# A max-pooling kernel whose first load becomes short and contiguous

## The chip, the cores and the metric

One core of a Trainium2 chip. The metric is the device time of one execution in microseconds. A profile has its own time, a little off the median of the others; where a profile is explained, its own time is used.

## The reference

```python
x: (32, 256, 4096) float32            # 134.2 MB
for i in range(256):                  # windows of 16 elements
    result[:, :, i] = np.max(x[:, :, 16*i : 16*i + 16], axis=-1)
# result: (32, 256, 256) float32      # 8.4 MB
```

Seen from one of the 128 partitions of the on-chip memory: 16,384 windows come in, 64 bytes each, and 16,384 floats go out.

## The kernel before

One area of 53,200 floats per partition holds three slots for loads, which shrink from the bottom up, and all results, which grow from the top down. So the stores can wait until every load has been issued. The loads and stores go through one queue, in program order. A load waits for the reduction that frees its slot.

```python
    AREA = 53200
    SLOTS = 3
    MOST = 65536 // (4 * W)          # 1024 windows: a row of 64 KB per partition
    ROUNDS_A = 3
    LAST = 4
    # ... sizes: three loads per round, as large as the room left allows
    # = 1024 x3, 980 x3, 924 x3, 868 x3, 816 x3, 768 x3, 244
    groups = [sizes[: ROUNDS_A * SLOTS], sizes[ROUNDS_A * SLOTS :]]
    # ...
    for g, loads in enumerate(groups):
        n = sum(loads)
        xg = xw[first : first + P * n].rearrange("(p n) w -> p (n w)", p=P)
        # ... cut: og, base, b
        for i, size in enumerate(loads):
            a = b - size
            at = n_loads % SLOTS * sizes[n_loads // SLOTS * SLOTS] * W
            slot = area[:, at : at + size * W]
            nc.sync.dma_start(out=slot, in_=xg[:, a * W : b * W])
            nc.vector.reduce_max(out=area[:, base + a : base + b], in_=..., axis=...)
        # ... stores: group 0 whole, group 1 in two parts
    for dst, src in stores:
        nc.sync.dma_start(out=dst, in_=src)
```

A *group* sets where the rows of a load lie in memory. A group of n windows per partition is one contiguous stretch, of which partition p owns n consecutive windows. A load takes a piece of each partition's share, so its 128 rows lie n × 64 bytes apart. In the first group of before n is 8784, so the rows lie 562,176 bytes apart.

## Time and profile before

| | before |
|---|---|
| time, median (range) | 335.48 us (335.36 to 335.57) |
| the profiled execution | 335.70 us, span 333.9 us |
| bytes moved | 134.22 MB read, 8.39 MB written |
| share of the DMA engines | 99.1% |
| VectorE busy | 276.0 us, 83% |

From the page of before: the line of the queue (packets, MB, share of sixteen engines), the bytes of the span, and the group of reductions (busy us, mean ns, idle time and what ended it).

```profile
q1 hardware_dynamic: 3168, 142.61, 99.1%
HBM read 134.22 MB, written 8.39 MB: 427 GB/s over the span
...
L75 DVE TENSOR_REDUCE area<-area 128x1024 f32<-128x16384 f32 (+6 forms) x19 | 276.0, 14525 | 50.0 <-DMA area<-in_x_dram 50.0
```

The transfers fill the span; VectorE is the one that waits. The table of stretches shows how fast they go (stretch, length, VectorE busy, POOL busy, TensorE clock, DMA share, GB/s):

```profile
0.00:23.00 23.00, 0.02 (x1) 0.20 (x4) 1.00 0.99 410
23.00:42.33 19.33, 17.20 (x2) 0.00 (x0) 1.00 1.00 434
300.00:313.00 13.00, 11.43 (x2) 0.00 (x0) 1.00 1.02 439
326.00:331.00 5.00, 0.00 (x0) 0.00 (x0) 1.00 0.95 404
```

A packet is counted in the stretch in which it starts, with its whole length, so short stretches are rough and can exceed 1.00. The second line is a whole load between two landings: 434 GB/s. The Trainium skill, "DMA: Bandwidth & Descriptors", section "Where 436 GB/s comes from", gives 435.2 GB/s as the ceiling of the sixteen ports to the on-chip memory; this trace, just under it, agrees. The same section also says that for transfers between the large memory (HBM) and the on-chip one a smaller ceiling of about 358 GB/s binds; this trace, of one core, does not show it: 434 GB/s.

The timeline of before, first three reductions and the last row (start, length, instruction, idle time before it):

```profile
22.98 17.22 DVE L75 TENSOR_REDUCE area<-area 128x1024 f32<-128x16384 f32 x1 [22.98 <-DMA area<-in_x_dram]
42.33 17.22 DVE L75 TENSOR_REDUCE area<-area 128x1024 f32<-128x16384 f32 x1 [2.13 <-DMA area<-in_x_dram]
61.68 17.22 DVE L75 TENSOR_REDUCE area<-area 128x1024 f32<-128x16384 f32 x1 [2.13 <-DMA area<-in_x_dram]
...
308.79 17.21 DVE L75 TENSOR_REDUCE area<-area 128x768 f32<-128x12288 f32 x2 [1.57 <-DMA area<-in_x_dram]
```

Landings come every 19.35 us, and a reduction of that size takes 17.22. So each reduction sits between two landings and never holds up a transfer.

Each of the sixteen DMA engines moves eight rows of a load. Once under way it takes 2.418 us for a 64 KB row, so eight take 19.34 us. The first reduction starts at 22.98 us, when the last of the sixteen engines has landed its share. 22.98 less 19.34 leaves 3.64 us. Of these, 1.77 us are no loss of an engine: 1.75 pass before the first packet (one row of one engine, as the trace records it) starts, and 0.02 between the last landing and the reduction. The other 1.87 us are the lateness: what the slowest engine lost at the start, its landing included.

### The profile page before, as it was taken

Reading aid. Unit: us, or ns where it says so; the run is one execution under the profiler, and the core shown is the slowest. Engines: PE = TensorE matmul, PEld = TensorE weight load, DVE = VectorE, ACT = ScalarE, POOL = GpSimd, SP = SyncE. Lnnn points to the kernel's source line nnn. Section 1 sums busy time; section 2 is a strip of 40 time slices with the busy share of each in tenths; the row PEclk is TensorE's granted clock in tenths of the full one; section 3 lists DMA queues with packets and bytes.
Section 4 is the critical chain, followed back from the end, with each engine's and each line's share of the span. In section 5 each row is a group of like instructions: output and inputs, shape, how many; then the busy total and the mean of one; then the engine's idle time right before and its main releaser. Section 6 shows DMA issues by size and latency. Waiting matters only on the chain.

```text
span 333.9 us, 109 instructions
## 1 busy us (share of the span) xinstructions
DVE 276.0 (83%) x19; POOL 0.2 (0%) x4
## 2 busy tenths in 40 slices
DVE  0029899798979899897979897979989798988990
POOL 0000000000000000000000000000000000000000
DMA  9898989998999998999999999999999998998997
GB/s 377 377 502 377 495 385 471 392 473 376 473 443 398 474 439 383 425 453 453 446 426 433 426 426 426 426 425 469 407 419 475 395 465 389 465 436 383 448 420 311
DMA packets 3168, 142.61 MB, mean 427 GB/s; under 512 B 352, under 2 KB 352, under 8 KB 352
## 3 DMA queue, kind: packets, MB, share of 16 engines
q1 hardware_dynamic: 3168, 142.61, 99.1%
HBM read 134.22 MB, written 8.39 MB: 427 GB/s over the span
## 4 chain that ended last, share of the span: by engine, by line
DMA 63%; DVE 34%; another core or an unknown queue 1%; issue 0%; SPq 0%
DMA area<-in_x_dram 63%; DVE area L75 34%; SPq L74 0%
## 5 line engine op out<-in xcount | busy, mean ns | idle before, releaser
L75 DVE TENSOR_REDUCE area<-area 128x1024 f32<-128x16384 f32 (+6 forms) x19 | 276.0, 14525 | 50.0 <-DMA area<-in_x_dram 50.0
L108 POOL MEMSET const-bfloat16-1.0<- 128x1 bf16 x1 | 0.1, 102 | 0.0
L108 POOL MEMSET const-uint8-127<- 128x1 uint8 x1 | 0.1, 101 | 0.0
L108 POOL MEMSET const-float32-0.0<- 128x1 f32 x1 | 0.1, 100 | 0.2 <-issue 0.2
L108 POOL MEMSET const-float32-1.0<- 128x1 f32 x1 | 0.1, 99 | 0.0
## 6 DMA issues: line engine op xcount, KB each, us to landing
area<-in_x_dram SPq DMA_DIRECT2D x3, 7840.0 KB, 39.1
area<-in_x_dram SPq DMA_DIRECT2D x3, 7392.0 KB, 36.9
area<-in_x_dram SPq DMA_DIRECT2D x3, 6944.0 KB, 34.7
area<-in_x_dram SPq DMA_DIRECT2D x3, 6528.0 KB, 32.6
area<-in_x_dram SPq DMA_DIRECT2D x3, 6144.0 KB, 30.7
out_dram<-area SPq DMA_DIRECT2D x1, 4392.0 KB, 30.7
out_dram<-area SPq DMA_DIRECT2D x1, 2526.0 KB, 36.3
area<-in_x_dram SPq DMA_DIRECT2D x1, 1952.0 KB, 20.7
```

The source lines that it names most:

```text
L75: nc.vector.reduce_max(out=area[:, base + a : base + b], in_=slot.rearrange("p (n w) -> p n w", w=W), axis=mybir.AxisListType.X,)
L108: nc = _bacc.Bacc("TRN2", target_bir_lowering=False, num_devices=1)
```

## The change

The intent, as the change reads: a first load of 320 windows (20 KB per partition) lets VectorE begin about 13 us earlier and frees the first slot earlier. The short load is made its own group, one contiguous stretch of 2.6 MB. That makes a fourth store. The rest of the sizes are laid out anew: 320, 1024 x2, 996 x3, 936 x3, 880 x3, 828 x3, 780 x3, 756.

```diff
+    FIRST = 320
 ...
-    sizes = []
-    left = total
+    slot_sizes = [MOST]
+    rounds = [[FIRST] + [MOST] * (SLOTS - 1)]
+    left = total - sum(rounds[0])
     while left:
         room = AREA - (total - left)
         n = min(room // (SLOTS * W + SLOTS) // ALIGN * ALIGN, MOST)
-        for _ in range(SLOTS):
+        if left <= slot_sizes[-1]:
+            n = left
+        slot_sizes.append(n)
+        rounds.append([])
+        while left and len(rounds[-1]) < SLOTS:
             n = min(n, left)
-            if n:
-                sizes.append(n)
-                left -= n
-    groups = [sizes[: ROUNDS_A * SLOTS], sizes[ROUNDS_A * SLOTS :]]
+            rounds[-1].append(n)
+            left -= n
+    sizes = [n for r in rounds for n in r]
+    groups = [sizes[:1], sizes[1 : ROUNDS_A * SLOTS], sizes[ROUNDS_A * SLOTS :]]
 ...
-            at = n_loads % SLOTS * sizes[n_loads // SLOTS * SLOTS] * W
+            at = n_loads % SLOTS * slot_sizes[n_loads // SLOTS] * W
 ...
-        if g == 0:
+        if g < len(groups) - 1:
 ...
-    for dst, src in stores:
+    for dst, src in stores[1:2] + stores[0:1] + stores[2:]:
```

## The prediction

> **What bounds the kernel now.** The transfers do. The DMA table gives one queue that fills 99.1% of the sixteen engines' span with 142.61 MB in 333.9 us. In the table of stretches, 23.0 to 42.3 us moves 434 GB/s at a DMA share of 1.00; later load stretches 430 to 436. The Trainium skill, "DMA: Bandwidth & Descriptors", section "Where 436 GB/s comes from", puts the ceiling at 435.2 GB/s; this trace agrees. VectorE is busy 276.0 us (83%): a 1024-window reduction takes 17.22 us against 19.35 us between two 64 KB-row landings. Its 50.0 us of idle time are waits for loads, 23.0 of them for the first. The chain of waits shows 63% loads and 34% reductions, but these reductions only let a load be issued behind one or two already queued; no queue runs dry, as the even landing intervals show.
>
> What is not streaming is small. First packets start at 1.77 us; the first 64 KB packet of an engine takes 2.84 to 3.80 us against 2.42 later, so about 1 us is lost once. After the last packet (332.5 us) come 0.5 us to landing and the program's end. About 2 us could be won at all, 0.6%.
>
> **What the change removes, adds, moves.** Bytes are the same. Loads stay 19, reductions 19, elements equal, so VectorE stays near 276 us. Sizes become 320, 2x1024, then threes of 996, 936, 880, 828, 780, and 756 last.
> - Start: the first load's rows are 45,056 bytes shorter; at 0.0367 ns a byte (from packets of 65,536 and 10,192 bytes: 2.418 and 0.387 us) and eight rows an engine, it lands 13.2 us earlier. First reduction near 9.8 us instead of 22.98. Off the critical path: loads 2 and 3 are queued in either kernel, and later loads still wait on reductions that keep ahead of the transfers.
> - The same two packet sizes give about 13 ns fixed cost per packet. The added store brings eight packets of 1,280 bytes to each engine: +0.1 us, on the critical path.
> - Tail: the last load lands at the same 313.5 us. Its reduction is now 756 windows, about 12.8 us, instead of 244 (4.2 us), but before it the 768-window one (12.95 us) was then just under way, so the last reduction ends near 326.3 us against 326.0. Stores queued behind the last load are 6.80 MB (6.92 before), about 15.8 us; the last store is ready 13.9 us after that landing (reduction plus the 1 us from issue to first packet seen at the start). Margin about 1.5 us: no gap.
> - The contiguous first stretch may shorten the 1 us at the start; I expect no more than a few tenths either way.
>
> Sum: +0.1 us, minus perhaps 0.2. Predicted 335.4 us, range 334.7 to 336.2. Chances: faster by over 2%: 0.01; within 2%: 0.98; slower by over 2%: 0.01.
>
> **What would show each step.** Timeline: first reduction at 9.5 to 10 us, last ending at 326 to 326.6. Last load's landing at 313.5 ± 0.7. DMA share still 99%; load stretches 430 to 436 GB/s. VectorE's first wait about 10 us, the 13 us it gains returning as longer waits for later loads (total idle near 50).
>
> **What would make it wrong.** A gap of the engines before the last store (stretches near 328 us below 0.9 share); a load issued too late because a shifted slot overlaps one still being read; a different rate for rows at the new distances in memory (load stretches off 430 to 436); or a start-up cost that depends on where and how long the first rows are, more than I assume.

## The result, and the profile after

| | before | after |
|---|---|---|
| time, median (range) | 335.48 (335.36 to 335.57) | 336.22 (335.70 to 336.53) |
| ratio to before, 95% interval | | 1.0021 (1.0008 to 1.0034) |
| the profiled execution, us | 335.70 | 336.06 |
| first reduction starts, us | 22.98 | 10.11 |
| less eight rows at their steady pace, us | 19.34 | 6.09 |
| lateness of the start, us | 1.87 | 2.24 |
| profiled time less lateness, us | 333.83 | 333.82 |

The profile of before (335.70 us) was slower than all its six timed runs, and that of after a little faster than its median, so the two latenesses understate the difference. Taking 333.8 us off the medians instead, an estimate, gives latenesses of about 1.7 and 2.4 us.

A ratio here is the mean time of one kernel's runs over that of the other's of the same rounds, so it is not quite the ratio of the medians. The changed kernel is the same by the 2% measure, and slower by 0.2%, with an interval that lies clear of 1. The median of 336.22 lies on the upper edge of the predicted range of 334.7 to 336.2, 0.02 above it as written.

The page of after, the same lines as shown of before:

```profile
q1 hardware_dynamic: 3312, 142.61, 98.9%
HBM read 134.22 MB, written 8.39 MB: 427 GB/s over the span
...
L82 DVE TENSOR_REDUCE area<-area 128x996 f32<-128x15936 f32 (+7 forms) x19 | 276.0, 14525 | 50.7 <-DMA area<-in_x_dram 50.7
```

The 144 new packets are one store's: 128 rows and 16 completion writes. Bytes and VectorE's work are as before. The stretches of after:

```profile
0.00:23.00 23.00, 5.49 (x1) 0.20 (x4) 1.00 0.95 402
23.00:42.33 19.33, 12.88 (x1) 0.00 (x0) 1.00 1.00 434
300.00:313.00 13.00, 12.68 (x1) 0.00 (x0) 1.00 0.95 412
326.00:331.00 5.00, 0.66 (x1) 0.00 (x0) 1.00 0.98 416
```

The steady rate is the same 434 GB/s, and there is no hole in front of the last store (326 to 331 us). The 412 in the third line comes from counting by starts, not from a lower rate: the last load's landing follows that of the load before by 14.30 us for 6.19 MB, which is 433 GB/s. The timeline of after:

```profile
10.11 5.49 DVE L82 TENSOR_REDUCE area<-area 128x320 f32<-128x5120 f32 x1 [10.11 <-DMA area<-in_x_dram]
29.45 17.22 DVE L82 TENSOR_REDUCE area<-area 128x1024 f32<-128x16384 f32 x1 [13.85 <-DMA area<-in_x_dram]
48.80 17.22 DVE L82 TENSOR_REDUCE area<-area 128x1024 f32<-128x16384 f32 x1 [2.13 <-DMA area<-in_x_dram]
...
313.90 12.75 DVE L82 TENSOR_REDUCE area<-area 128x756 f32<-128x12096 f32 x1 [1.22 <-DMA area<-in_x_dram]
```

VectorE begins 12.87 us earlier and waits 13.85 us for the second load instead of 2.13. The head start is handed back at once, since VectorE was not what the kernel waited for. The last reduction ends at 326.65 us against 326.00.

Now the small loss. The prediction put the first landing at 22.98 − 13.2, about 9.8 us; it came at 10.11. From the first load's last landing to the last store's, the trace has 323.32 us after and 310.03 before. The 13.29 us between these are, but for 0.03 us, the eight rows' shortening (8 × (2.418 − 0.761) = 13.26). So all that is lost is lost before the first load has landed. The trace's landing records show how: the sixteen engines' landings of the first load span 1.46 us (0.99 before), and this spread stays to the end of the program (1.47 us in the last store). So does the gap between the last landing and the one before it: 0.61 us in the first load, 0.62 in the last store. Each engine moves its eight rows of every transfer, and in these traces nothing evens the engines out. The slowest one ends the program.

### The profile page after: what moved, and what is told of

Read it like the earlier page. It is cut to its first block, busy times and chain, and to the rows that moved or that the text cites. A ratio compares the mean times of both kernels' runs of the same rounds, so it can differ in the third digit from the quotient of the medians.

```text
span 334.3 us, 110 instructions
## 1 busy us (share of the span) xinstructions
DVE 276.0 (83%) x19; POOL 0.2 (0%) x4
## 4 chain that ended last, share of the span: by engine, by line
DMA 65%; DVE 31%; another core or an unknown queue 0%; SPq 0%; issue 0%; DVEq 0%
DMA area<-in_x_dram 65%; DVE area L82 31%; SPq L81 0%; DVEq L82 0%
## 5 line engine op out<-in xcount | busy, mean ns | idle before, releaser
L82 DVE TENSOR_REDUCE area<-area 128x996 f32<-128x15936 f32 (+7 forms) x19 | 276.0, 14525 | 50.7 <-DMA area<-in_x_dram 50.7
```

Source lines behind the costliest of these rows:

```text
L82: nc.vector.reduce_max(out=area[:, base + a : base + b], in_=slot.rearrange("p (n w) -> p n w", w=W), axis=mybir.AxisListType.X,)
```

## The experiments

After the first profile there were three theories: *short start* (short first rows let the engines begin further apart), *contiguous start* (the one stretch of memory does it), and *store and tail* (the fourth store or the larger last reduction cost it). All times below are medians, with ratios against runs of before on the same chip. "Lateness" is read from the profile of each run.

| run | rows of first load, distance | median us | ratio (95%) | lateness us | profiled us less lateness |
|---|---|---|---|---|---|
| before | 64 KB, 562,176 B | 335.48 | | 1.87 | 333.83 |
| after | 20 KB, 20,480 B | 336.22 | 1.0021 (1.0008 to 1.0034) | 2.24 | 333.82 |
| e1_short_strided | 20 KB, 522,496 B | 335.50 | 1.0001 (0.9987 to 1.0014) | 1.64 | 333.85 |
| e2_long_contig | 64 KB, 65,536 B | 335.37 | 0.9995 (0.9983 to 1.0008) | 1.70 | 333.75 |
| e3_split_store | 64 KB, 562,176 B | 335.52 | 1.0001 (0.9988 to 1.0013) | 1.66 | 333.84 |
| e4_after_again | 20 KB, 20,480 B | 335.95 | 1.0013 (1.0000 to 1.0025) | 2.03 | 333.82 |
| e5_first_324 | 20.25 KB, 20,736 B | 335.85 | 1.0009 (0.9997 to 1.0022) | 1.96 | 333.87 |
| e6_first_512 | 32 KB, 32,768 B | 335.46 | 0.9997 (0.9984 to 1.0011) | 1.59 | 333.80 |
| e7_pair_group | 20 KB, 86,016 B | 335.16 | 0.9989 (0.9977 to 1.0002) | 1.34 | 333.78 |
| e8_short_second | 64 KB, 65,536 B | 335.27 | 0.9991 (0.9979 to 1.0004) | 1.38 | 333.75 |
| e9_long_close | 64 KB, 20,480 B | 336.10 | 1.0016 (1.0004 to 1.0029) | 2.11 | 333.79 |
| e10_first_128 | 8 KB, 8,192 B | 335.21 | 0.9991 (0.9979 to 1.0004) | 1.39 | 333.80 |
| e11_pair_again | 20 KB, 86,016 B | 335.29 | 0.9993 (0.9979 to 1.0007) | 1.59 | 333.79 |
| e12_pitch_40k | 20 KB, 40,960 B | 335.43 | 0.9999 (0.9986 to 1.0011) | 1.80 | 333.82 |

The last column is the main finding: in fourteen profiles of twelve programs, time less lateness stays within 333.75 to 333.87 us, while the times themselves range from 335.12 to 336.06. Number of stores (three to five), of loads (19 or 20), sizes and tails differ among them and hardly count.

The late versions stand apart in time too. All 21 timed runs of after, e4_after_again, e5_first_324 and e9_long_close took 335.70 us or more; of the 78 of before and the other versions one did (335.84, of before). This is firmer than the single ratios, since those of e4_after_again and e5_first_324 have intervals that reach 1.

### e1_short_strided

The short first load without its own group and without the fourth store.

```diff
-    groups = [sizes[:1], sizes[1 : ROUNDS_A * SLOTS], sizes[ROUNDS_A * SLOTS :]]
+    groups = [sizes[: ROUNDS_A * SLOTS], sizes[ROUNDS_A * SLOTS :]]
-    for dst, src in stores[1:2] + stores[0:1] + stores[2:]:
+    for dst, src in stores:
```

> The changed kernel with its short first load put back into the first group of loads (rows 500 KB apart instead of one contiguous stretch) and so without the fourth store. Theory 'short start' (short first rows let the sixteen engines begin further apart, and the last of them sets the end): still slow, 336.0 to 336.4 us, ratio to before 1.0015 to 1.0025, spread of the first load's sixteen landings about 1.4 us. Theory 'contiguous start' (the one stretch of memory does it): back to 335.3 to 335.6, spread 1.0 us. Theory 'store and tail' (the fourth store costs it): back to 335.3 to 335.6, with the spread of the landings without a bearing on the time.

Measured: 335.50 us, spread of the first landings 0.68 us. The first row of its timeline:

```profile
9.50 5.49 DVE L82 TENSOR_REDUCE area<-area 128x320 f32<-128x5120 f32 x1 [9.50 <-DMA area<-in_x_dram]
```

The same load lands 0.61 us earlier than in after. *Short start* alone falls.

### e2_long_contig

```diff
-    FIRST = 320
+    FIRST = 1024
```

> The changed kernel with a first load of 1024 windows: all load sizes are then those of before, but the first load still is a contiguous stretch of its own and its results still have a fourth store. 'Short start': 335.5 to 335.7 us (only the 0.1 us of the extra packets), landings of the first load 1.0 us apart. 'Contiguous start': 336.0 to 336.4, landings about 1.4 us apart. 'Store and tail': 336.0 to 336.4, landings 1.0 us apart.

Measured: 335.37 us, spread 0.75 us. *Contiguous start* alone falls, and so does *store and tail*: the fourth store is here, and the larger last reduction was in e1_short_strided, neither of them late.

### e3_split_store

```diff
-            stores.append((og, area[:, base : base + n]))
+            c = n - 320
+            for a, b in ((0, c), (c, n)):
+                stores.append((og[:, a:b], area[:, base + a : base + b]))
```

> The kernel before with its first store cut in two (8464 and 320 columns), nothing else: the cost of a fourth, short store alone. 'Store and tail': 336.0 to 336.4 us. Both start theories and the sum of the prediction: +0.1 us, 335.5 to 335.7, ratio about 1.0003.

Measured: 335.52 us. From the first load's last landing to the last store's the trace has 310.10 us against 310.03 of before: the short store costs 0.07 us in this pair of profiles.

### e4_after_again

No edit.

> The changed kernel unaltered, for a second profile and more times. All theories: 335.7 to 336.5 us again, ratio near 1.002. Start theories: the spread of the first load's landings is again over 1.2 us, and if this profile's time differs from the first one's 336.06, the lateness of the first load's last landing differs by the same amount; 'store and tail' expects no such link.

Measured: 335.95 us, spread 1.31 us. The profile took 335.85 us, 0.21 less than the first one's 336.06, and its lateness is 2.03 us, 0.21 less than 2.24. The link holds to the hundredth. The loss is there again, though smaller in the median; it varies from run to run.

After these four, only short and contiguous *together* were late. What sets that combination apart is that the first rows lie close: 128 rows within 2.6 MB. *Close rows* was the new theory. *Pitch* was its rival: the distance of 20,480 bytes is a multiple of 4,096.

### e5_first_324

```diff
-    FIRST = 320
+    FIRST = 324
```

> First load of 324 windows, contiguous: its rows lie 20,736 bytes apart (256 times 81) instead of 20,480 (4,096 times 5). So far, time minus the lateness of the first load's last landing (landing after the first packet's start, less eight rows at their steady 2.418 or 0.761 us) is 333.8 us in six profiles, and only short and contiguous together are late. 'Close rows' (the first rows all lie within 2.6 MB): slow as the changed kernel, 335.8 to 336.4 us, lateness 2.0 to 2.4 us. 'Pitch' (the distance 20,480, a multiple of 4,096, makes engines meet in the memory): 335.4 to 335.6, lateness 1.6 to 1.9.

Measured: 335.85 us, lateness 1.96. Still slow by its times, though at the low edge of what *close rows* expected and just under in lateness, which is near the 1.87 of the profile of before; *pitch* as the sole cause falls.

### e6_first_512

```diff
-    FIRST = 320
+    FIRST = 512
```

> First load of 512 windows, contiguous: 32 KB rows, 32,768 bytes apart, all within 4.2 MB. 'Close rows': between the 20 KB and the 64 KB version, 335.5 to 336.0 us, lateness 1.8 to 2.1 us. 'Pitch': 32,768 is a higher power of two than either, so as slow or slower than the changed kernel, 336 us or more, unless the long-row version (65,536, not slow) speaks against it already.

Measured: 335.46 us, lateness 1.59. Not between, as *close rows* expected, but as good as any: at 32 KB apart nothing is lost against before. *Pitch* falls once more.

### e7_pair_group

```diff
-    groups = [sizes[:1], sizes[1 : ROUNDS_A * SLOTS], sizes[ROUNDS_A * SLOTS :]]
+    groups = [sizes[:2], sizes[2 : ROUNDS_A * SLOTS], sizes[ROUNDS_A * SLOTS :]]
```

The changed kernel with the first two loads in one group: the same sizes and number of transfers, but the 20 KB rows, and those of the second load, now lie 86,016 bytes apart. The first stores are divided otherwise.

> First load of 320 windows as in the changed kernel, but in one group with the second load: its 20 KB rows lie 86,016 bytes apart (4,096 times 21), within 11 MB, not contiguous. Sizes and number of loads and stores unchanged. 'Close rows': 335.4 to 335.6 us, lateness 1.6 to 1.8 as with rows 500 KB apart. 'Pitch': 336.0 to 336.4, lateness over 2.0 (the power of two in the distance is the same as with 20,480).

Measured: 335.16 us, lateness 1.34, spread 0.45. This is faster than either theory expected. One line of grouping takes back the loss and more. The first rows of its timeline, and the last:

```profile
9.17 5.49 DVE L82 TENSOR_REDUCE area<-area 128x320 f32<-128x5120 f32 x1 [9.17 <-DMA area<-in_x_dram]
28.51 17.22 DVE L82 TENSOR_REDUCE area<-area 128x1024 f32<-128x16384 f32 x1 [13.85 <-DMA area<-in_x_dram]
...
312.96 12.75 DVE L82 TENSOR_REDUCE area<-area 128x756 f32<-128x12096 f32 x1 [1.22 <-DMA area<-in_x_dram]
```

Against after, the first reduction is 0.94 us earlier, the second 0.94, the last 0.94, and the profiled time 0.94 us lower (335.12 against 336.06). What is lost in the first microseconds is neither regained nor added to.

### e8_short_second

```diff
-    rounds = [[FIRST] + [MOST] * (SLOTS - 1)]
+    rounds = [[MOST, FIRST] + [MOST] * (SLOTS - 2)]
-    groups = [sizes[:1], sizes[1 : ROUNDS_A * SLOTS], sizes[ROUNDS_A * SLOTS :]]
+    groups = [sizes[:1], sizes[1:2], sizes[2 : ROUNDS_A * SLOTS], sizes[ROUNDS_A * SLOTS :]]
-    for dst, src in stores[1:2] + stores[0:1] + stores[2:]:
+    for dst, src in stores[2:3] + stores[0:2] + stores[3:]:
```

> The changed kernel with its short contiguous load second, behind a contiguous 64 KB-row load, both groups of their own (five stores). 'Cold start only' (short close rows hurt only while the engines start): 335.3 to 335.6 us, and the second load's landings lie no further apart than the first's. 'Always' (any such load spreads the engines): 335.9 to 336.4, the second load's landings over 0.3 us further apart than the first's.

Measured: 335.27 us; the landings spread over 0.51 us in the first load and 0.48 in the second. The same 20 KB contiguous rows cost nothing once the engines run: *cold start only*.

### e9_long_close

Wrong result (relative error 0.10): e2_long_contig with the first load's 64 KB rows read 20,480 bytes apart, so that they overlap in memory.

```diff
-            nc.sync.dma_start(out=slot, in_=xg[:, a * W : b * W])
+            src = xg[:, a * W : b * W]
+            if n_loads == 0:
+                src = bass.AP(tensor=src.tensor, offset=0, ap=[[320 * W, P], [1, size * W]])
+            nc.sync.dma_start(out=slot, in_=src)
```

> Wrong result on purpose. The version with a contiguous 64 KB-row first load, but the rows of that load are read 20,480 bytes apart (overlapping in memory), so its first rows lie as close as the changed kernel's and are as long as the kernel before's; all sizes, stores and the work after it unchanged. 'Closeness alone': 335.8 to 336.4 us, lateness of the first load's last landing 2.0 to 2.4 us, as the changed kernel. 'Short and close together': 335.3 to 335.6, lateness 1.4 to 1.8, as with rows 64 KB apart.

Measured: 336.10 us, ratio clear of 1, lateness 2.11 us, spread 1.21 us. First row of its timeline, then that of e2_long_contig, which differs by the distance and, with it, the overlap:

```profile
23.21 17.22 DVE L85 TENSOR_REDUCE area<-area 128x1024 f32<-128x16384 f32 x1 [23.21 <-DMA area<-in_x_dram]
```

```profile
22.80 17.22 DVE L82 TENSOR_REDUCE area<-area 128x1024 f32<-128x16384 f32 x1 [22.80 <-DMA area<-in_x_dram]
```

At this distance 64 KB rows are late as well, so it does not take short rows. One rival stays: rows that overlap read the same bytes up to four times, and no run separates that from the distance. In after nothing overlaps, and it is as late. How the engines start can be seen in stretches of the first 3 us, the first packets of before, then of e9_long_close (all are 64 KB):

```profile
1.70:2.20 0.50, 0.00 (x0) 0.00 (x0) 1.00 6.63 2097
2.20:2.40 0.20, 0.00 (x0) 0.00 (x0) 1.00 0.00 0
2.40:3.03 0.63, 0.00 (x0) 0.00 (x0) 1.00 0.00 0
```

```profile
1.70:2.20 0.50, 0.00 (x0) 0.00 (x0) 1.00 4.48 1573
2.20:2.40 0.20, 0.00 (x0) 0.00 (x0) 1.00 0.00 0
2.40:3.03 0.63, 0.00 (x0) 0.00 (x0) 1.00 1.16 416
```

A packet counts where it starts: 2097 GB/s over 0.5 us is 16 packets of 65,536 bytes: all engines of before start within that half microsecond. In e9_long_close 12 do (1573), and four only after 2.4 us (416 GB/s over 0.63 us). The packet records add that three of these four follow the rest by little, while one is 0.62 us behind the next slowest after eight rows. In after it is also one engine that trails, by 0.63 us, and in e4_after_again, by 0.54; in e5_first_324 none trails alone (0.28). The sixteen engines' *mean* lateness is 1.23 us in after and 1.35 in before: on average the engines of after lose no more. One engine does, and the program waits for it.

Late starts alone do not make a late version. In e1_short_strided, which is not late, four engines also start only after 2.4 us (130 GB/s over 0.63 us is four packets of 20,480 bytes):

```profile
1.70:2.20 0.50, 0.00 (x0) 0.00 (x0) 1.00 1.74 410
2.20:2.40 0.20, 0.00 (x0) 0.00 (x0) 1.00 0.73 205
2.40:3.03 0.63, 0.00 (x0) 0.00 (x0) 1.00 0.43 130
```

Its last engine starts at 2.71 us. Followed from packet to packet, the trailing engine starts at 2.85 us in e9_long_close and at 3.12 in after, about 0.4 us behind all others. In e4_after_again it starts at 2.44 us, among others, but its first row takes 1.80 us, the longest of the sixteen.

### e10_first_128

```diff
-    FIRST = 320
+    FIRST = 128
```

> First load of 128 windows, contiguous: 8 KB rows within 1 MB, 20 loads (0.1 us more of packets). Closeness, whether alone or with short rows: at least as late as the changed kernel, lateness 2.0 us or more, 336.0 us or more, since the rows are closer still. If only the region of 2.6 MB or the length of 20 KB is special: 335.4 to 335.7.

Measured: 335.21 us, lateness 1.39, spread 0.39. This is a miss for *close rows* as it was put: rows 8,192 bytes apart, closer still, are not late. So it is not simply "the closer, the worse"; of the distances tried, 20,480 and 20,736 bytes are late, and 8,192 and those from 32,768 up are not. At 8,192 the rows are shorter too; no run has long rows that close.

### e11_pair_again

No edit to e7_pair_group.

> The version of the paired first group (20 KB rows 86,016 bytes apart) again, unaltered: is it really faster than the kernel before? If so 335.1 to 335.3 us and a ratio of 0.999 again, lateness 1.3 to 1.5. If the first run drew a lucky start: 335.4 to 335.6, lateness 1.6 to 1.9.

Measured: 335.29 us, lateness 1.59 in its profile. The median lies where "really faster" expected it, the lateness between the two expectations. All ten timed runs of this version (335.12 to 335.40) lie below all runs of before taken beside them (335.43 and up), but both intervals of the ratio reach 1. All runs of e8_short_second and e10_first_128 lie below theirs as well, so the pairing is nothing special. The paired version beats the changed kernel; that it beats the kernel before, by some 0.1%, is likely and not settled.

### e12_pitch_40k

```diff
-    rounds = [[FIRST] + [MOST] * (SLOTS - 1)]
+    rounds = [[FIRST, FIRST] + [MOST] * (SLOTS - 2)]
-    groups = [sizes[:1], sizes[1 : ROUNDS_A * SLOTS], sizes[ROUNDS_A * SLOTS :]]
+    groups = [sizes[:2], sizes[2 : ROUNDS_A * SLOTS], sizes[ROUNDS_A * SLOTS :]]
```

> Two first loads of 320 windows in one group: 20 KB rows 40,960 bytes apart, within 5.2 MB; 20 loads (0.1 us more of packets). Closeness with its limit between 2.6 and 4.2 MB: 335.3 to 335.7 us, lateness 1.3 to 1.7. If short rows need more room than long ones: 335.9 or more, lateness 1.9 or more.

Measured: 335.43 us, lateness 1.80. By its time not late; its profile (335.62) was the slowest of its five runs, and 1.80 is over the 1.7 expected and under the 1.9 of the other side. It does not tell more than that 40,960 bytes are not as bad as 20,480.

## Why the prediction was right or wrong

- *The transfers bound the kernel.* Right. 434 GB/s and about 99% in both profiles, and the 12.87 us that VectorE gains at the start come back as 13.85 us of waiting for the second load.
- *The earlier start is off the critical path, so the time hardly moves.* Right: +0.2% by the ratio.
- *The added store costs 0.1 us.* Right in size: e3_split_store shows 0.07 us.
- *No gap at the tail, though the last reduction is three times as long.* Right. The last reduction ended at 326.65 us (326.3 predicted, 326.6 the most expected); nearly all of the difference is that of the first landing, 10.11 us against about 9.8.
- *"The contiguous first stretch may shorten the 1 us at the start; I expect no more than a few tenths either way", booked as "minus perhaps 0.2".* This term failed, in sign and size. In the profiles the start lost 0.37 us against before (2.24 against 1.87), and in the medians the changed kernel is 0.5 us (e4_after_again) to 0.7 us behind. The text had named this among the things that could make it wrong. What the runs showed in its place: with the first rows 20 KB apart one engine (in e5_first_324 not one alone) falls behind at its start, and since shares are fixed, the slowest one's delay goes in full to the end. e9_long_close (against e2_long_contig, distance and overlap changed: +0.44 us in the profile) and the paired group (against after, distance raised to 86,016 bytes: −0.94 and −0.68 in its two profiles) show it from both sides.
- *Range.* The first median, 336.22 us, came out on its upper edge, the second, 335.95, inside. The sum itself, 335.4 us, expected no loss; the range had room for one, and that is as much width as insight.

What is shown is that the loss arises before the first load has landed, that it stays to the end, and that it goes with rows 20 KB apart in the first load. What stays open: why 20,480 and 20,736 bytes are late and 8,192 is not. The trace shows packets and landings, not where in memory or on the way there an engine is held up. Each version has one or two profiles, and the lateness of the same kernel moves by 0.2 us between profiles (2.24 and 2.03; 1.34 and 1.59), so differences among the good versions are not read as effects of the distance.

## What to carry to other kernels

In a kernel whose transfers run at the ceiling from end to end, as here, giving the compute engine an earlier start buys nothing; look for what the transfers wait on, or leave it. What was left to win or lose here sat in the first microseconds: a load split over sixteen engines was as late as the slowest of them, and with equal shares its delay at the start was paid at the end. Subtract the steady streaming time from the first landing and compare that remainder between versions: here it explained differences of 0.9 us in 335 to within about 0.1 us.

## What the Trainium skill lacked or had wrong

- "DMA: Bandwidth & Descriptors", section "Why a DMA increments its semaphore by 16 and not by 1": it says that the engines of a transfer finish independently and that only the full count means landed. These runs agree (spreads of 0.4 to 1.5 us in one load) and add what is not there: in a long stream the spread of the first load persists to the last store (1.46 and 1.47 us in after), so here the worst start set the end of the program.
- The same page, section "Latency and other measured facts", has a row on the row pitch at large powers of two, from 512 KiB up. It has nothing on small distances at the start of a program: rows 20,480 or 20,736 bytes apart gave a lateness of 1.96 to 2.24 us and medians of 335.85 to 336.22, other distances 1.34 to 1.87 and 335.16 to 335.52. Rows 65,536 bytes apart, a power of two below those of the page, lost nothing against before (e2_long_contig, lateness 1.70).
- Another row of that section gives about 600 ns to the first byte for transfers issued from the sync queue. In before about 1.0 us pass from the start of the issue (0.73 us) to the start of the first packet (1.75 us), and the first row of an engine then takes 0.4 to 1.4 us longer than its later ones.
